# Thirteen u tiles instead of nine ahead of the gate matmuls, and a third, moved buffer for spilled activations

## The chip, the core and the metric

The kernel is one program on one core of a Trainium2 chip. Its engines run side by side and each works through its own instructions in order: TensorE (PE; its weight loads are PEld), VectorE (DVE), ScalarE (ACT), GpSimd (POOL) and SyncE (SP, which issues most DMAs). Engines wait for each other and for DMAs by semaphores. A DMA issued by ScalarE or GpSimd stands in that engine's order too. The metric is the device time of one execution in microseconds; shown are a median over runs and one execution with a profile.

## The reference

Two layers over 512 tokens of width 1024: a recurrent block, then attention, each followed by an expert layer ("PEER"). The expert layer picks 16 of 128 x 128 single-neuron experts per head and token and sums them:

```python
def peer(h, w_q, sub_keys, u_tab, v_tab):
    q = (h @ w_q).reshape(B, S, PEER_HEADS, 2, PEER_HALF)
    s = jnp.einsum('bshpd,hpnd->bshpn', q, sub_keys).astype(jnp.float32)
    v1, i1 = lax.top_k(s[..., 0, :], PEER_TOPK)
    v2, i2 = lax.top_k(s[..., 1, :], PEER_TOPK)
    cand = (v1[..., :, None] + v2[..., None, :]).reshape(B, S, PEER_HEADS, PEER_TOPK * PEER_TOPK)
    cv, ci = lax.top_k(cand, PEER_TOPK)
    ...
    idx = e1 * N_KEYS + e2
    g = jax.nn.softmax(cv, axis=-1).astype(h.dtype)
    def experts(args):
        hc, ic, gc = args
        act = jax.nn.gelu(jnp.einsum('bcd,bchkd->bchk', hc, u_tab[ic]), approximate=False)
        return jnp.einsum('bchk,bchkd->bcd', gc * act, v_tab[ic])
```

There are 8 heads, 128 keys, 16384 experts per layer, and everything is float32.

## The kernel before, in words

The expert layer treats the 512 tokens in two ways. For the last block of 128 tokens it gathers the chosen rows of the tables u and v, one choice per step: an indirect DMA on GpSimd's queue (L1113) fills a buffer `grow` (four of them), VectorE takes the dot product with the token (L1117) or adds the weighted row (L1120, L1122). There are 256 such steps per layer, `total`; `done` counts those emitted. For the other three blocks (384 tokens) it computes all 16384 experts densely and multiplies them with a matrix of gate weights that is zero where an expert was not chosen.

A u tile is 128 experts: its weights are loaded by SP into `raw` (four buffers), ScalarE rounds them to `whi` and VectorE takes the rest `wlo` (three buffers each, shared with `vh` and `vl` of the second half), TensorE makes 8 x 3 matmuls of 384 columns into one of two PSUM banks named `u` (L187 to L189), and ScalarE applies the gelu into SBUF. Of the 128 tiles the first 8 go into the space of x, tiles 8 to 16 and those from 93 on stay in SBUF, and tiles 17 to 92 (`SPILL` = 76) are spilled: the gelu writes a small tile `gsp` (L895), and ScalarE issues a DMA of it to scratch memory `gscr` (L896), from which SP fetches it in the second half (L1035).

An expert layer runs in these stages.

- Queries, scores and top-k, four groups; after each group some u tiles (`UPQ`), 23 in all. The last block's indices are decoded first, so that the gathers can begin.
- `UDEC` u tiles, with `FIRST` gather steps spread among them, while VectorE decodes the three dense blocks. When block 0 is decoded, three transposes into `et` (L808) bring its indices and weights into the gate layout.
- 24 gate groups of 16 tokens. VectorE builds one-hot tiles `oo` and weighted ones `pr` (L835, L837, two buffers each), TensorE multiplies them into PSUM `wps` (L843), ScalarE evicts four banks into `stg` (L846) and issues the DMA to `wscr` (L848). The u tiles up to number 88 and the gather steps up to `EARLY` are spread over the groups, as is the decoding of blocks 1 and 2.
- `UEND` = 5 more u tiles.
- The second half: for each of the 128 tiles t, `weigh` multiplies the activation with its gate weights and splits it (`ah`, `al`), `v_load` loads and splits v (`vh`, `vl`), and TensorE adds 18 matmuls into the six banks `acc` (L187 to L189 again). Gate weights come from `wscr` as `wt`, for eight tiles at a time, two buffers (L993); tiles 0 and 1 use a small tile `wfirst` (L989). The u tiles from 93 on and the remaining gather steps run among the tiles; all gather steps are spread by weights from `done` to `total`.

The order on each engine is made by a scheduler, from the order of the source, priorities and its own timeline of the instructions. Tiles live in pools that lie on a stack: `gath` (gpool), `cg`, and above them `dec` (dpool), with the pool of the current stage on top. `dec.close()` frees dpool after the first half, and the pool `vp` of the second half (`wt`, `ah`, `al`) is laid over the freed space; a tile there waits until what lay in its place has been read. gpool stays to the end of the layer.

Of the kernel before, what the change touches and what calls it, by code (L numbers as in the profile page):

```python
# [9 lines left out]
F32 = mybir.dt.float32  # L10
# [11 lines left out]
P = 128  # L22
# [17 lines left out]
ND = 3 * P  # L40
# [2 lines left out]
SPILL = 76  # L43
LEAD = KC + RING - 3 + SPILL
UPQ = (5, 6, 6, 6)
UDEC = 9
UEND = 5
FIRST = 12
EARLY = 100
HT = 8  # L50
RAWS = 4
GROWS = 4
# [29 lines left out]
class Trunk:  # L82
# [768 lines left out]
    def peer(self, l):  # L851
        nc, io, tc = self.nc, self.io, self.tc
        nd = NB - 1
        with ExitStack() as st:
# [28 lines left out]
            def u_part(after=None):  # L883
                t = state["u"]
                state["u"] = t + 1
                out = self.bank("u", True)
                hi, lo = self.wtile(io["uT"][l][t], KC, eng=nc.vector)
                with tc.issue_after(after) if after is not None else ExitStack():
                    for k, (bh, bl) in enumerate(h):
                        self.mm3(out[:, :ND], (hi[:, k, :], lo[:, k, :]), (bh[:, :ND], bl[:, :ND]), k == 0, k == KC - 1)  # L890
                if t < KC:
                    gact[t] = self.x[:, t, :ND]
                elif LEAD - SPILL <= t < LEAD:
                    g = gpool.tile([P, ND], F32, name="gsp", bufs=2)
                    nc.scalar.activation(g, out[:, :ND], AF.Gelu)  # L895
                    nc.scalar.dma_start(self.gscr[l, t - (LEAD - SPILL)], g)  # L896
                    return
                else:
                    gact[t] = acts.tile([P, ND], F32, name="gact")
                nc.scalar.activation(gact[t], out[:, :ND], AF.Gelu)  # L900

            gpool = st.enter_context(tc.tile_pool(name=f"gath{l}", bufs=1))
# [7 lines left out]
            dpool = dec.enter_context(tc.tile_pool(name=f"dec{l}", bufs=1))  # L910

            def decodes(bs):
                for b in bs:
                    res = []
                    for _ in self.decode(dpool, cvs[b], cis[b], iu[b], res):
                        yield
                    if b == nd:
                        gsel.append(self.gather_index(gpool, l, *res))
                    else:
                        prep[b] = self.gate_prep(pool, *res)  # L920

            with tc.tile_pool(name=f"pq{l}", bufs=1) as pool:
                for grp in range(4):
# [29 lines left out]
                    for _ in range(UPQ[grp]):  # L953
                        u_part()
            with tc.tile_pool(name=f"gate{l}", bufs=1) as pool:
                nsg = P // TG
                steps = decodes(range(nd))
                for i in range(UDEC):
                    u_part()
                    while done < FIRST * (i + 1) // UDEC:  # L960
                        next(gsteps)
                        done += 1
                while 0 not in prep:
                    next(steps)
                n0, nt = state["u"], nd * nsg
                ds = 0
                wlast = [None, None]
                for i in range(nt):
                    while state["u"] < n0 + (LEAD - UEND - n0) * (i + 1) // nt:
                        u_part(after=wlast[-2])  # L970
                    wlast.append(self.gate_group(pool, l, i // nsg, i % nsg, *prep[i // nsg]))
                    while ds < 7 * (i + 1) // nsg:
                        next(steps, None)
                        ds += 1
                    while done < min(EARLY, FIRST + (EARLY - FIRST) * (i + 1) // (nt - 2)):
                        next(gsteps)
                        done += 1
                while state["u"] < LEAD:
                    u_part(after=wlast[-1])
# [248 lines left out]
```

## Time and profile before

| | |
|---|---|
| median of three runs | 3194.11 us (3189.2 to 3195.05) |
| the profiled execution | 3191.91 us, its span 3190.1 us |
| mean granted TensorE clock | 0.973 |
| TensorE, VectorE, ScalarE, GpSimd busy | 3003.0, 2582.8, 1379.5, 859.8 us |
| DMA | 821.13 MB, 257 GB/s over the span |

Layer 0's expert layer lies from about 213 us to 1531 us of the span, layer 1's from about 1857 us to 3167 us. A busy share is an average over stages with different limits, so the stages are read apart. In a row on waits, what stands before the arrow waited, and what stands behind it ended the wait; in a timeline row, the bracket at the end holds the idle time before an instruction and what ended it.

### The profile page before, as it was taken

How to read it: one execution, taken by the hardware profiler on the slowest of the kernel's cores; microseconds unless marked ns; L12 is line 12 of the kernel's file. 1: busy time of each engine (PE TensorE's matmuls, PEld its weight loads, DVE VectorE, ACT ScalarE, POOL GpSimd, SP SyncE). 2: the span in 40 equal slices, each digit the busy share in tenths (PEclk: the TensorE clock that was granted, in tenths of full speed). 3: DMA queues.
4: the chain of work that ended last, by engine and by line, in shares of the span. 5: the costliest groups of instructions: out<-in, count | busy, mean ns of one | idle time of the engine just before them, and what ended most of it. 6: DMA issues, size and time to landing. Idle time of an engine off the chain costs nothing.

```text
span 3190.1 us, 43195 instructions
## 1 busy us (share of the span) xinstructions
PE 3003.0 (94%) x15334; PEld 2633.5 (83%) x15334; DVE 2582.8 (81%) x4927; ACT 1379.5 (43%) x1960; POOL 859.8 (27%) x653
## 2 busy tenths in 40 slices
PE   6999987999999999999889889969998999999997
PEld 5659987998877889998667679969998788889996
DVE  8859999987788877878578878998986677778776
ACT  5533244655333333333566542445554333333333
POOL 0000014433122114443356500034333111124440
PEclk9999998999999999999999999989999999999999
DMA  7444578998999999998113244479998999999994
GB/s 287 148 161 139 176 240 296 343 321 301 316 333 359 350 337 317 329 334 284 52 50 112 67 156 130 150 263 329 335 314 297 308 319 301 313 310 333 319 324 142
DMA packets 345110, 821.13 MB, mean 257 GB/s; under 512 B 33600, under 2 KB 179136, under 8 KB 338496
## 3 DMA queue, kind: packets, MB, share of 16 engines
q1 hardware_dynamic: 239632, 460.91, 43.7%
q0 software_dynamic: 73728, 268.47, 24.2%
q10 hardware_dynamic: 31536, 89.00, 7.4%
q8 instruction: 121, 1.98, 0.2%
q14 instruction: 93, 0.76, 0.1%
HBM read 730.98 MB, written 87.29 MB: 257 GB/s over the span
## 4 chain that ended last, share of the span: by engine, by line
PE 77%; DVE 11%; DMA 4%; ACT 4%; issue 3%; POOL 1%; ACTq 0%; SPq 0%; DVEq 0%; POOLq 0%
PE acc L187 10%; PE acc L188 10%; PE acc L189 10%; PE u L187 10%; PE u L188 9%; PE u L189 9%; PE wps L843 5%; PE pq L187 2%; PE pq L189 2%; PE pq L188 2%; DVE wlo L163 1%; PE wo L207 1%; DMA grow<-in_u_dram,idx 1%; ACT stg L846 1%; DVE ada_junk L151 1%
## 5 line engine op out<-in xcount | busy, mean ns | idle before, releaser
L1113 POOL DMA_INDIRECT grow<-in_u_dram,idx x256 | 340.6, 1330 | 1416.8 <-DVE oh L791 704.1
L187 PE MATMUL u<-hh,wlo 128*128 128x384 f32 x2048 | 696.4, 340 | 21.7 <-ACT gsp L895 21.7
L189 PE MATMUL u<-hh,whi 128*128 128x384 f32 x2048 | 692.3, 338 | 0.0
L188 PE MATMUL u<-hl,whi 128*128 128x384 f32 x2048 | 691.5, 338 | 0.0
L188 PE MATMUL acc<-vl,ah 128*128 128x512 f32 x1536 | 601.0, 391 | 0.4 <-DVE vl L163 0.4
L189 PE MATMUL acc<-vh,ah 128*128 128x512 f32 x1536 | 600.6, 391 | 0.0
L187 PE MATMUL acc<-vh,al 128*128 128x512 f32 x1536 | 563.5, 392 | 12.4 <-ACT vh L162 7.5
L1113 POOL DMA_INDIRECT grow<-in_v_dram,idx x256 | 350.9, 1371 | 680.0 <-DVE gacc L1122 467.9
L163 DVE TENSOR_TENSOR vl<-vraw,vh 128x1024 fp32r<-128x1024 f32 x256 | 313.5, 1225 | 194.3 <-ACT vh L162 189.0
L163 DVE TENSOR_TENSOR wlo<-raw,whi 128x1024 fp32r<-128x1024 f32 x307 | 376.8, 1227 | 112.7 <-ACT whi L162 105.8
L162 ACT ACTIVATE whi<-raw 128x1024 fp32r<-128x1024 f32 (+2 forms) x364 | 350.1, 963 | 220.3 <-PE u L189 128.8
L187 PEld LDWEIGHTS u<-hh,wlo 128*128 128x128 f32 x2048 | 389.5, 190 | 29.9 <-ACT gsp L895 27.0
L188 PEld LDWEIGHTS u<-hl,whi 128*128 128x128 f32 x2048 | 389.1, 190 | 2.9
L189 PEld LDWEIGHTS u<-hh,whi 128*128 128x128 f32 x2048 | 388.6, 190 | 0.0
L187 PEld LDWEIGHTS acc<-vh,al 128*128 128x128 f32 x1536 | 289.9, 189 | 73.2 <-ACT vh L162 8.9
L189 PEld LDWEIGHTS acc<-vh,ah 128*128 128x128 f32 x1536 | 289.5, 189 | 60.6
L188 PEld LDWEIGHTS acc<-vl,ah 128*128 128x128 f32 x1536 | 289.5, 188 | 59.8 <-DVE vl L163 0.8
L162 ACT ACTIVATE ah<-gact 128x384 fp32r<-128x384 f32 x240 | 125.8, 524 | 483.8 <-PE acc L189 308.6
L1117 DVE CUSTOM_DVE_ANT_0 grow<-grow,hn 128x1024 f32<-128x1024 f32 x256 | 308.8, 1220 | 31.1 <-DMA grow<-in_u_dram,idx 31.0
L1122 DVE SCALAR_TENSOR_TENSOR gacc<-grow,gdot,gacc 128x1024 f32<-128x1024 f32 x254 | 325.2, 1280 | 1.6 <-DMA grow<-in_v_dram,idx 0.6
L162 ACT ACTIVATE vh<-vraw 128x1024 fp32r<-128x1024 f32 x256 | 268.9, 1050 | 117.6 <-issue 45.3
L846 ACT ACTIVATE stg<-wps 128x512 f32<-128x512 f32 x192 | 190.9, 1094 | 70.8 <-PE wps L843 66.8
(337 smaller groups left out, 4232.1 us busy)
## 6 DMA issues: line engine op xcount, KB each, us to landing
raw<-in_uT_dram SPq DMA_DIRECT2D x256, 512.0 KB
vraw<-in_v_dram SPq DMA_DIRECT2D x256, 512.0 KB
ada_raw<-in_adaw_dram SPq DMA_DIRECT2D x112, 512.0 KB
wscr<-stg ACTq DMA_DIRECT2D x48, 1024.0 KB
wt<-wscr SPq DMA_DIRECT2D x32, 1536.0 KB
gscr<-gsp ACTq DMA_DIRECT2D x152, 192.0 KB
gact<-gscr SPq DMA_DIRECT2D x152, 192.0 KB
raw<-in_w_pq_dram SPq DMA_DIRECT2D x32, 512.0 KB
```

Source lines behind the costliest of these rows:

```text
L151: nc.vector.tensor_tensor_reduce(junk, raw, self.csil, op0=OP.mult, op1=OP.add, scale=1.0, scalar=b, accum_out=col)
L162: nc.scalar.activation(hi, src, AF.Copy)
L163: return (eng or nc.vector).tensor_tensor(lo, src, hi.bitcast(F32), op=OP.subtract)
L187: nc.tensor.matmul(out, al, bh, start=first, stop=False)
L188: nc.tensor.matmul(out, ah, bl, start=False, stop=False)
L189: return nc.tensor.matmul(out, ah, bh, start=False, stop=last)
L207: self.nc.tensor.matmul(outs[m], ws[k][:, m, :], acts[k], start=k == 0, stop=k == KC - 1)
L843: last = nc.tensor.matmul(wps[:, t * P:t * P + P], oo[:, n4 + a, :, t], pr[:, q * n4 + a, :, t], start=q == 0, stop=q == 1)
L846: nc.scalar.activation(stg[:, :, c:c + 4].rearrange("p e t -> p t e"), wps.rearrange("p (t e) -> p t e", t=4), AF.Copy, scale=1.0 / GSCALE)
L1113: nc.gpsimd.indirect_dma_start(out=row, out_offset=None, in_=tabs[s], in_offset=bass.IndirectOffsetOnAxis(ap=idx[:, k:k + 1], axis=0))
L1117: nc.vector.tensor_tensor_reduce(row, row, hn, op0=OP.mult, op1=OP.add, scale=1.0, scalar=0.0, accum_out=col)
L1122: nc.vector.scalar_tensor_tensor(acc, row, col, acc, op0=OP.mult, op1=OP.add)
```

## The change

Nine u tiles between the scores and the gate matmuls become thirteen (`UDEC`), and the u tiles that remain for the gate groups are four fewer. Of the gather steps, 4 and not 12 are asked for in that place (`FIRST`), and 94 and not 100 up to the end of the gate groups (`EARLY`), so six more per layer fall into the second half. The tile `gsp` has three buffers and not two, and they are taken from dpool and not from gpool.

```diff
-UDEC = 9
+UDEC = 13
 UEND = 5
-FIRST = 12
-EARLY = 100
+FIRST = 4
+EARLY = 94
...
                 elif LEAD - SPILL <= t < LEAD:
-                    g = gpool.tile([P, ND], F32, name="gsp", bufs=2)
+                    g = dpool.tile([P, ND], F32, name="gsp", bufs=3)
                     nc.scalar.activation(g, out[:, :ND], AF.Gelu)
                     nc.scalar.dma_start(self.gscr[l, t - (LEAD - SPILL)], g)
                     return
```

How this moves instructions shows at three places. The first lies between the scores and the gate groups of layer 0. On ScalarE (`et` and `gt` are the transposed indices and weights of block 0, the first thing that the gates need):

```order
+L794 ACTIVATE ib<-i4f 128x1024
+L895 ACTIVATE gsp<-u 128x384
+L162 ACTIVATE whi<-raw 128x1024
+L896 DMA gscr<-gsp 128x384
 L811 ACTIVATE et<-et 128x2x16x8
 L814 ACTIVATE gt<-et 128x128
```

Four such triples of gelu, rounding and scratch write now stand ahead of `et`; on TensorE the u tiles between the last score and the first gate matmul go from 19 to 23 in either layer, and some three of them stand between the transposes of `et`. On VectorE, at the same place (`e` is the decoded index for which these transposes wait, L1117 a gather step):

```order
 L773 SCALAR_TENSOR_TENSOR off<-row,off 128x128
-L800 TENSOR_TENSOR e_4019<-oh 128x64
-L1117 ISA grow,gdot<-grow,hn 128x1024
-L1117 ISA gdot 128x1
+L163 TENSOR_TENSOR wlo<-raw,whi 128x1024
+L1117 ISA grow,gdot<-grow,hn 128x1024
+L1117 ISA gdot 128x1
+L800 TENSOR_TENSOR e_4131<-oh 128x64
 L791 TENSOR_TENSOR oh<-iota_m,rc 128x1024
```

The split of a new u tile and a gather step stand ahead of `e` now. Up to the first gate product, VectorE has four splits more; the gather steps ahead of it are 15 where they were 16 in layer 0, and 15 as before in layer 1.

The second place is ScalarE in the last third of layer 0's gate groups. Before:

```order
L162 ACTIVATE whi<-raw 128x1024 x2
L846 ACTIVATE stg<-wps 128x4x128 x2
L895 ACTIVATE gsp<-u 128x384
L846 ACTIVATE stg<-wps 128x4x128 x2
L896 DMA gscr<-gsp 128x384
L895 ACTIVATE gsp<-u 128x384
L848 DMA wscr<-stg 128x2048
L896 DMA gscr<-gsp 128x384
```

and with the change:

```order
L895 ACTIVATE gsp<-u 128x384
L162 ACTIVATE whi<-raw 128x1024
L846 ACTIVATE stg<-wps 128x4x128
L896 DMA gscr<-gsp 128x384
L846 ACTIVATE stg<-wps 128x4x128 x3
L848 DMA wscr<-stg 128x2048
L895 ACTIVATE gsp<-u 128x384
```

Before, two roundings stand together ahead of the evictions and the gelus behind them; now gelu and rounding alternate up to the end of the gate groups, as they did before in the first two thirds.

The third place is the passage to the second half of layer 0, on ScalarE, with what each row waits for in brackets (DMAHW0 to DMAHW7 count landed DMAs, the others an engine's instructions). Before:

```order
L895 ACTIVATE gsp<-u 128x384 [waits DMAHW5_49]
L896 DMA gscr<-gsp 128x384 [waits Activation_49]
L162 ACTIVATE ah<-x 128x384 [waits DVE_49]
L162 ACTIVATE vh<-vraw 128x1024 [waits DMAHW4_49,PE_49]
```

and with the change:

```order
L162 ACTIVATE vh<-vraw 128x1024 [waits DMAHW1_49,DVE_49,PE_49]
L895 ACTIVATE gsp<-u 128x384 [waits DMAHW2_49]
L896 DMA gscr<-gsp 128x384 [waits Activation_49]
L162 ACTIVATE ah<-x 128x384 [waits DMAHW4_49,DMAHW1_49,DMAHW7_49,DMAHW0_49,DVE_49]
L162 ACTIVATE ah<-x 128x384 [waits DVE_49]
```

Before, the first `ah` stood ahead of the last two `gsp` and waited for VectorE alone. Now it stands behind the last one, and three of the DMAs it waits for are scratch writes of `gsp`, the last tile's among them. On SP, the first load of `wt` waited for the last gate matmul, and now for the last `gsp` and its scratch write as well, before:

```order
L993 DMA wt<-wscr 128x24x128 [waits DMAHW0_49,PE_49]
L993 DMA wt<-wscr 128x24x128 [waits DMAHW1_49]
```

and with the change:

```order
L993 DMA wt<-wscr 128x24x128 [waits DMAHW1_49,DMAHW0_49,DMAHW5_49,PE_49,Activation_49]
L993 DMA wt<-wscr 128x24x128 [waits DMAHW6_49]
```

The second `wt` load of each pair follows the first in either program.

## The prediction, on record before the changed kernel was timed

> **What bounds the kernel now.** I read the page first, then the busy times by stage, then the waits, then the two places where a wait stands on TensorE.
>
> ```profile
> span 3190.1 us, 43195 instructions
> PE 3003.0 (94%) x15334; PEld 2633.5 (83%) x15334; DVE 2582.8 (81%) x4927; ACT 1379.5 (43%) x1960; POOL 859.8 (27%) x653
> PE 77%; DVE 11%; DMA 4%; ACT 4%; issue 3%; POOL 1%; ACTq 0%; SPq 0%; DVEq 0%; POOLq 0%
> ```
>
> TensorE is busy for 94% of the span and is 77% of the chain that ended last, so the time is its work plus its holes. Next, the first half of each expert layer by stages: from the last score to the first gate matmul (388.4 to 499.7 in layer 0, 2033 to 2137.4 in layer 1), the gate matmuls, and the u tiles after the last of them up to the first output matmul; columns are length, then busy time of each engine, granted clock, DMA share, GB/s.
>
> ```profile
> core 0: us, PE busy (x) PEld busy (x) DVE busy (x) ACT busy (x) POOL busy (x), PEclk, DMA share, GB/s
> 388.40:499.70 111.30, 79.88 (x458) 78.98 (x458) 104.93 (x359) 47.02 (x60) 25.49 (x20) 0.86 0.71 232
> 499.70:813.00 313.30, 306.87 (x1975) 299.63 (x1975) 270.87 (x311) 171.63 (x209) 122.50 (x75) 0.97 0.91 319
> 813.00:838.60 25.60, 21.44 (x121) 20.48 (x119) 14.30 (x15) 8.89 (x12) 7.55 (x6) 1.00 1.03 338
> 2033.00:2137.40 104.40, 80.02 (x458) 78.90 (x457) 100.03 (x351) 45.28 (x58) 22.43 (x19) 0.91 0.68 225
> 2137.40:2450.00 312.60, 306.66 (x1974) 298.27 (x1973) 267.29 (x307) 174.19 (x210) 117.46 (x74) 0.98 0.90 317
> 2450.00:2490.00 40.00, 28.77 (x145) 27.81 (x144) 19.19 (x19) 10.11 (x14) 12.12 (x10) 0.91 1.00 336
> ```
>
> Before the first gate matmul VectorE is the bound (104.9 of 111.3 us, 100.0 of 104.4) and TensorE stands still for 31.4 and 24.4 us. In the gate stage it is the other way round, TensorE 306.9 of 313.3 us. The waits name the holes; columns are total, times, longest.
>
> ```profile
> PE et L808 <- DVE e L800: 33.1, 4, 13.3
> PE wps L843 <- DVE pr L837: 22.5, 2, 12.4
> PE u L187 <- ACT gsp L895: 21.7, 17, 2.6
> ```
>
> The first two rows, 55.6 us, are the holes before the gates: the transposes wait for the decoded indices, the first gate matmul for its one-hot product. The third is spread over the last third of the gates and the u tiles behind them: a u tile waits until the gelu of an earlier one has emptied its PSUM bank.
>
> **Term A, the hole before the gates.** What one u tile and one gather cost:
>
> ```profile
> 412.00:462.00 50.00, 50.00 (x290) 50.00 (x289) 5.91 (x12) 1.00 0.69 216
> L163 DVE TENSOR_TENSOR wlo<-raw,whi 128x1024 fp32r<-128x1024 f32 x19 | 23.5, 1235 | 0.0
> L1117 DVE CUSTOM_DVE_ANT_0 grow<-grow,hn 128x1024 f32<-128x1024 f32 x16 | 19.4, 1215 | 5.2 <-DMA grow<-in_u_dram,idx 5.2
> L1122 DVE SCALAR_TENSOR_TENSOR gacc<-grow,gdot,gacc 128x1024 f32<-128x1024 f32 x254 | 325.2, 1280 | 1.6 <-DMA grow<-in_v_dram,idx 0.6
> ```
>
> The first row counts u matmuls alone: 290 in 50 us, 0.172 us each, 24 to a tile, so 4.14 us; four more tiles put 16.6 us of work into each hole. They also put four splits of 1.24 us, 4.9 us, on VectorE ahead of the first gate product. The table asks for eight fewer gathers there, but the order takes one out in layer 0 (16 to 15) and none in layer 1 (15 to 15): the gathers fill places that the scheduler has free anyway. So the first gate matmul comes 4.9 - 1.2 = 3.7 us later in layer 0 and 4.9 us later in layer 1, and the gate stage has 16.6 us less to do: a gain of 12.9 + 11.7 = 24.6 us. Bounds: 33.2 us if VectorE takes the splits in its own idle 6.4 and 4.4 us; 14 us if each new split costs twice its time because its load comes late (the gather row shows 5.2 us of such waits). I take the middle, since VectorE is 94 to 96% busy there, and its idle is in waits for the first gathers.
>
> **Term B, the late gates.** The gate stage after the change holds 290 us of TensorE work and, with 75 gather steps down to 70 (74 to 71) and a split less, 263 us of VectorE work: 91%, where it was 86%. An early stretch of it, then the late ones:
>
> ```profile
> 520.00:680.00 160.00, 160.00 (x1047) 157.12 (x1046) 145.09 (x174) 94.38 (x115) 69.44 (x39) 1.00 0.94 336
> 720.00:813.00 93.00, 86.57 (x541) 83.05 (x540) 72.93 (x74) 47.43 (x58) 27.61 (x21) 0.93 0.87 299
> 2360.00:2450.00 90.00, 84.09 (x523) 80.48 (x521) 68.94 (x72) 44.91 (x55) 29.16 (x20) 0.94 0.85 297
> 794.51 2.80 ACT L846 ACTIVATE stg<-wps 128x512 f32<-128x512 f32 x3
> 797.72 0.49 ACT L895 ACTIVATE gsp<-u 128x384 f32<-128x384 f32 x1 [0.40 <-ACT stg L846]
> 798.26 0.69 PE L187 MATMUL u<-hh,wlo 128*128 128x384 f32 x1 [2.50 <-ACT gsp L895]
> ```
>
> With VectorE at 91% from 520 to 680, TensorE had no hole, and DMA went at 336 GB/s; so the denser gates can hold. The late ones have holes although VectorE has slack: the gelu at 797.72 stands behind three evictions of gate banks on ScalarE, and TensorE waits 2.50 us for it. In the new order each gelu stands directly behind its tile to the end of the stage, as it stood in the stretch without holes. Of the 21.7 us of these waits nearly all lie here. The clock adds to it: 0.93 over 93 us, 0.94 over 90 and 0.91 over 40 us make 2 x (0.07 x 93 + 0.06 x 90 + 0.09 x 40) = 31 us at half rate; with some 12 of them idle, 19 us of work at half rate lose 9. Together 30 us; against it I put 5 us of new holes per layer for the fuller VectorE. B is a gain of 20 us, bounds 30 and 0 (as many new holes as old ones).
>
> **Term C, the passage to the second half.** Here the moved buffer costs. The second half's pool lies where the decode pool was. In the new program the first load of gate weights (wt) and the first split of an activation (ah) wait for the scratch write of the last spilled tile; before, they stood ahead of it. The last gelu itself stands behind the third vh, which waits for the last u matmul. Rows that carry it:
>
> ```profile
> 838.63 1.66 PE L187 MATMUL acc<-vh,al 128*128 128x512 f32 x6 [1.15 <-ACT vh L162]
> 844.21 0.97 PE L187 MATMUL acc<-vh,al 128*128 128x512 f32 x3 [1.20 <-ACT vh L162]
> 2490.02 1.22 PE L187 MATMUL acc<-vh,al 128*128 128x512 f32 x2 [5.16 <-ACT vh L162]
> L162 ACT ACTIVATE vh<-vraw 128x1024 fp32r<-128x1024 f32 x256 | 268.9, 1050 | 117.6 <-issue 45.3 <-DMA vraw<-in_v_dram 24.5 <-PE acc L189 23.0
> 2477.73 0.33 ACTq L896 DMA_DIRECT2D gscr<-gsp  x1
> 2045.72 2.21 DMA gscr<-gsp
> SPq L1035 <- DMA gscr<-gsp: 24.6, 6, 7.0
> L163 DVE TENSOR_TENSOR al<-gact,ah 128x384 fp32r<-128x384 f32 x240 | 135.1, 563 | 71.4 <-ACT ah L162 71.0 <-issue 0.2
> L998 DVE TENSOR_TENSOR gact<-gact,wt 128x384 f32<-128x384 f32 x240 | 132.6, 552 | 0.0
> 2462.62 25.79 DMA wt<-wscr
> 2600.00:2700.00 100.00, 100.00 (x443) 82.81 (x442) 0.00 (x0) 0.00 (x0) 1.00 0.93 309
> ```
>
> Now 1.15 + 1.20 and 5.16 us are lost. After, counted from the end of the last u tile: vh 1.05, gelu 0.49, issue 0.33, the write between 2.2 us (the chain) and 7.0 us (the longest wait of SP for one), where I take 4.5, then ah and al, 0.5 to 0.6 each: the first output matmul at about 8 us. Tiles 0 and 1 need no wt and last 2 x 18 matmuls of 0.226 us (443 in 100 us), 8.1 us, to 16 us. The wt load starts at 6.4 us. Its price lies between 4.7 us (1536 KB at the 336 GB/s above) and 25.8 us (the chain's piece, two loads and gathers together); I take 11, near half of that piece. Behind it come the product 0.55, ah and al, a split and a gather that stand between on VectorE: tile 2 at about 21 us, a second hole of 4 to 5 us. With 2 us at half rate that is 14 us per layer, 28 in all, against 7.5 us and some 1.5 us of slow clock now: a loss of 19 us. Bounds: 5.2 us per layer and no second hole, a loss of 2; or 10 + 20 + 4 us per layer, a loss of 59. The near end is likelier than the far one, which counts two loads for one.
>
> [...]
>
> **Term D, the second half.** Six gather steps per layer move there, 1.22 to 1.28 us each on VectorE and 512 KB of DMA.
>
> ```profile
> 838.60:1530.80 692.20, 685.72 (x3202) 591.18 (x3203) 556.98 (x756) 255.64 (x345) 201.02 (x156) 0.99 0.94 326
> 2490.00:3167.10 677.10, 677.08 (x3178) 585.22 (x3179) 514.43 (x662) 246.74 (x337) 182.99 (x154) 1.00 0.89 302
> ```
>
> VectorE has 135 and 163 us idle here and TensorE none, so 7.5 us per layer hide under TensorE; without that cover they would cost 15. Layer 0 is denser (326 GB/s, 6.5 us of holes already): I put 1 us, bounds 0 and 5. The rest of the program differs by a few exchanged neighbours; I price it at nothing.
>
> **Sum.** -24.6 - 20 + 19 + 1 = -24.6 us, from the profiled execution's 3191.9 us to 3167.3, so 3167. The median shown is 2.2 us above that execution, the three runs reach from 3189.2 to 3195.05.
>
> **The rivals.** First, the passage eats the gain and more. It is one mechanism: wt cannot start before the last scratch write, lands late among gathers and v loads, and all output matmuls from tile 2 stand behind it. At the far bound: 3191.9 - 24.6 - 20 + 59 + 1 = 3207. It turns the result slower once the holes exceed 26 us per layer. For it: the 25.8 us piece. Against: that piece held two loads of wt, three of v and gathers. Second, the gates keep their pace: if VectorE in order sets it, the 16.6 us taken out of TensorE there become holes. Then A is a loss of 8.6 (the later first gate) and B a gain of 10 (the tail's waits): 3192 + 8.6 - 10 + 19 + 1 = 3210. For it: VectorE at 91%. Against: at 91% it held TensorE full from 520 to 680, and its own waits there are for TensorE. Third, the passage is cheap and the late gates close fully: 3191.9 - 24.6 - 30 + 2 + 1 = 3140. For it: the 2.21 us write.
>
> **How the numbers follow.** The forecast (3153 to 3187) has 0.65, the cheap passage (below 3153) 0.17, the dear passage 0.11, the gates that keep their pace 0.07. The bounds of A and C reach over 3143 to 3190, which leaves out the far ends of three rivals, about 2 in 10. A measurement of this kernel tells no less than 0.2%, 6.4 us, from no change. Faster by more: forecast, cheap passage and a fifth of the dear one's cases, 0.84; the rest of that one and the slow gates are split into 0.07 within and 0.09 slower.
>
> **What would show it.** A: the first gate matmul 3 to 5 us later after the last score, 23 u tiles before it and not 19, TensorE's hole there 18 and 13 us. B: the wait of u for gsp below 5 us in all, the clock near 1.00 up to the last gate. C: the first output matmul waits about 8 us behind the last u tile and a second hole stands before the third v tile, with ah or wt behind the scratch write as releaser. D: no new hole after that. A hole before a gate product in the middle of the stage would prove B wrong, a passage under 5 us or over 25 us C.

## The result, and the profile after

The changed kernel takes 3175.0 us (median of 5 runs, 3172.0 to 3175.4); the kernel before took 3194.1 us beside it (5 runs, 3189.0 to 3202.0). The ratio is 0.9931, 95% interval 0.9917 to 0.9945: faster by 0.7%, and 8 us slower than the 3167 forecast, inside its range of 3153 to 3187. The page of the changed kernel, span and busy times:

```profile
span 3171.8 us, 43218 instructions
PE 2997.4 (95%) x15334; PEld 2626.9 (83%) x15334; DVE 2585.5 (82%) x4927; ACT 1377.0 (43%) x1960; POOL 860.7 (27%) x653
```

The same work, 18.3 us less span than before. Busy times by stage, with the columns as in the prediction: the stage before the gates, the gates, the u tiles up to the first output matmul, for layer 0 and layer 1; then the second halves, and last the attention part between the layers:

```profile
386.90:502.10 115.20, 96.71 (x554) 95.50 (x553) 108.20 (x362) 50.87 (x66) 26.51 (x19) 0.94 0.72 248
502.10:799.70 297.60, 293.06 (x1928) 287.20 (x1928) 260.27 (x302) 170.55 (x208) 113.09 (x69) 0.99 0.92 319
799.70:832.90 33.20, 20.81 (x120) 20.50 (x119) 20.20 (x21) 9.28 (x14) 11.05 (x7) 0.85 0.93 314
2028.10:2136.60 108.50, 96.22 (x554) 95.39 (x554) 104.21 (x354) 50.93 (x66) 24.14 (x19) 0.96 0.72 249
2136.60:2437.70 301.10, 292.63 (x1928) 286.86 (x1928) 261.93 (x304) 170.12 (x208) 109.47 (x69) 0.98 0.90 318
2437.70:2468.70 31.00, 20.80 (x121) 20.51 (x120) 18.80 (x19) 9.47 (x14) 12.81 (x10) 0.88 0.92 304
832.90:1517.00 684.10, 676.31 (x3154) 580.43 (x3155) 557.51 (x757) 252.75 (x338) 207.90 (x162) 1.00 0.94 331
2468.70:3148.70 680.00, 675.77 (x3154) 582.94 (x3155) 514.42 (x664) 242.29 (x331) 188.69 (x159) 0.99 0.89 306
1517.00:1851.50 334.50, 287.66 (x1337) 217.89 (x1335) 258.97 (x473) 193.50 (x405) 165.01 (x134) 0.92 0.23 76
```

and the attention part of the kernel before:

```profile
1530.80:1856.80 326.00, 279.32 (x1337) 213.50 (x1335) 253.66 (x473) 192.87 (x405) 166.26 (x134) 0.94 0.25 78
```

From the last score to the last output matmul, layer 0 took 1142.4 us and takes 1130.1 (386.9 to 1517.0); layer 1 took 1134.1 and takes 1120.6. That is -25.7 us in the layers the change touches, where the forecast had -24.6. The attention part, which it doesn't touch, took 326.0 us and takes 334.5: +8.5 us, and with 1 us less elsewhere the span's 18.3.

TensorE's waits, as totals, times and longest in us:

```profile
PE wps L843 <- DVE pr L837: 31.8, 8, 9.9
PE acc L187 <- DVE al L163: 30.6, 8, 12.4
```

No wait of u for gsp is left (21.7 us before). The waits of et and of the first product fell with the two holes before the gates, from 31.4 and 24.4 us to 18.5 (115.2 less 96.7) and 12.3 (108.5 less 96.2). Eight waits of acc for al, 30.6 us, stand where two of 4.9 us stood, 28.2 us of them in four holes at the two passages. New are waits for pr in the middle of the gates, the largest of them here with VectorE's rows just before it:

```profile
2246.63 3.60 PE L843 MATMUL wps<-pr,oo 128*128 128x128 f16 x29 [8.23 <-DVE pr L837]
...
2241.46 0.28 DVE L818 TENSOR_TENSOR gp<-gt,gp 128x128 f16<-128x128 f32 x1
...
2242.80 1.22 DVE L1117 CUSTOM_DVE_ANT_0 grow<-grow,hn 128x1024 f32<-128x1024 f32 x1
...
2244.14 1.22 DVE L1117 CUSTOM_DVE_ANT_0 grow<-grow,hn 128x1024 f32<-128x1024 f32 x1
...
2245.40 2.33 DVE L837 TENSOR_TENSOR pr<-oo,gp 128x2048 f16<-128x2048 f16 x2
```

This is the switch from block 0 to block 1: the first product of block 1 needs its weights `gp`, which are decoded, transposed and ready at 2241.7. VectorE has no idle time of over half a microsecond in the ten before the product, and a split and two gather steps stand between `gp` and it. In all kernels of this document the holes of over 1.3 us before gate products, after the first product, stand at such a switch, 101 to 112 us or 206 to 225 us after the first gate matmul; the one exception is 2.4 us long, in the change with two buffers. In the kernel before, the four switches take 8.9 to 12.3 us from the last product of one block to the first of the next, and u matmuls fill them; in the changed kernel they take 11.2 to 16.8 us, and the u matmuls leave holes of 2.8, 1.1, 8.2 and 0.2 us in them. Late in the gates, where the waits for gsp had been, TensorE is now full at full clock:

```profile
720.00:799.70 79.70, 79.15 (x527) 77.22 (x527) 65.84 (x71) 44.34 (x54) 24.68 (x17) 1.00 0.92 318
2360.00:2437.70 77.70, 77.70 (x520) 75.81 (x519) 64.67 (x69) 43.98 (x54) 23.07 (x17) 1.00 0.92 327
```

The passage of layer 1, in order of time by engine (TensorE, ScalarE, VectorE, SP); a bracket is the idle time before and what ended it:

```profile
2468.68 0.76 PE L187 MATMUL acc<-vh,al 128*128 128x512 f32 x1 [10.20 <-DVE al L163]
2482.70 0.80 PE L187 MATMUL acc<-vh,al 128*128 128x512 f32 x1 [4.22 <-DVE al L163]
...
2459.99 0.33 ACTq L896 DMA_DIRECT2D gscr<-gsp  x1
2464.27 0.94 ACT L162 ACTIVATE ah<-x 128x384 fp32r<-128x384 f32 x2 [4.31 <-DMA gscr<-gsp]
...
2460.75 2.60 DVE L1122 SCALAR_TENSOR_TENSOR gacc<-grow,gdot,gacc 128x1024 f32<-128x1024 f32 x2
2463.27 1.02 DVE L998 TENSOR_TENSOR x<-x,wfirst 128x384 f32<-128x384 f32 x2
2464.20 1.28 DVE L1122 SCALAR_TENSOR_TENSOR gacc<-grow,gdot,gacc 128x1024 f32<-128x1024 f32 x1
2466.82 1.29 DVE L1122 SCALAR_TENSOR_TENSOR gacc<-grow,gdot,gacc 128x1024 f32<-128x1024 f32 x1 [1.34 <-DMA grow<-in_v_dram,idx]
2468.03 1.02 DVE L163 TENSOR_TENSOR al<-x,ah 128x384 fp32r<-128x384 f32 x2
2478.35 1.03 DVE L998 TENSOR_TENSOR x<-x,wt 128x384 f32<-128x384 f32 x2 [9.30 <-DMA wt<-wscr]
...
2464.22 8.25 SPq L993 DMA_DIRECT2D wt<-wscr  x2
```

The last u matmul ends at 2458.5. The scratch write of the last spilled tile is issued at 2460.0 and frees ah 4.3 us later. But two gather steps on VectorE keep the weighting of tile 0, which ah needs too, until 2463.8, so without the write ah could have come less than half a microsecond sooner. Then al does not follow: two more gather steps stand ahead of it on VectorE, the second waiting 1.34 us for its row. The wt load is issued at 2464.2, and its product starts at 2478.35, 14.1 us later, so the third tile finds a second hole. Layer 0 has holes of 12.41 and 1.41 us, and there ah waits for VectorE alone (ScalarE's row, then VectorE's):

```profile
827.08 0.99 ACT L162 ACTIVATE ah<-x 128x384 fp32r<-128x384 f32 x2 [5.10 <-DVE x L998]
...
823.98 2.60 DVE L1122 SCALAR_TENSOR_TENSOR gacc<-grow,gdot,gacc 128x1024 f32<-128x1024 f32 x2
826.50 1.02 DVE L998 TENSOR_TENSOR x<-x,wfirst 128x384 f32<-128x384 f32 x2
...
831.06 1.28 DVE L1122 SCALAR_TENSOR_TENSOR gacc<-grow,gdot,gacc 128x1024 f32<-128x1024 f32 x1 [2.35 <-DMA grow<-in_v_dram,idx]
832.26 1.02 DVE L163 TENSOR_TENSOR al<-x,ah 128x384 fp32r<-128x384 f32 x2
```

As in layer 1, two gather steps stand ahead of the weighting of tiles 0 and 1, and two more between it and al, here with a wait of 2.35 us for a row.

### The profile page after: what moved, and what is told of

It reads as the page before. It is cut to its first block, busy times and chain, and to the rows that moved or that the text cites. A ratio compares the mean times of both kernels' runs of the same rounds, so it can differ in the third digit from the quotient of the medians.

```text
span 3171.8 us, 43218 instructions
## 1 busy us (share of the span) xinstructions
PE 2997.4 (95%) x15334; PEld 2626.9 (83%) x15334; DVE 2585.5 (82%) x4927; ACT 1377.0 (43%) x1960; POOL 860.7 (27%) x653
## 4 chain that ended last, share of the span: by engine, by line
PE 74%; DVE 11%; issue 6%; DMA 5%; ACT 2%; POOL 2%; DVEq 0%; SPq 0%; POOLq 0%; ACTq 0%
PE acc L187 10%; PE acc L188 10%; PE acc L189 10%; PE u L187 9%; PE u L188 9%; PE u L189 9%; PE wps L843 5%; PE pq L187 2%; PE pq L188 2%; PE pq L189 2%; DVE wlo L163 1%; PE wo L207 1%; DMA ada_raw<-in_adaw_dram 1%; DMA grow<-in_u_dram,idx 1%; DVE grow L1117 1%
## 5 line engine op out<-in xcount | busy, mean ns | idle before, releaser
L187 PE MATMUL acc<-vh,al 128*128 128x512 f32 x1536 | 573.7, 392 | 33.4 <-DVE al L163 30.6
L187 PEld LDWEIGHTS acc<-vh,al 128*128 128x128 f32 x1536 | 289.5, 189 | 96.7 <-issue 23.8
L1122 DVE SCALAR_TENSOR_TENSOR gacc<-grow,gdot,gacc 128x1024 f32<-128x1024 f32 x254 | 324.8, 1279 | 9.8 <-DMA grow<-in_v_dram,idx 8.5
L1117 DVE CUSTOM_DVE_ANT_0 grow<-grow,hn 128x1024 f32<-128x1024 f32 x256 | 309.1, 1219 | 25.8 <-DMA grow<-in_u_dram,idx 25.6
L843 PE MATMUL wps<-pr,oo 128*128 128x128 f16 x1536 | 190.5, 297 | 31.8 <-DVE pr L837 31.8
```

The costliest lines, as they stand in the source:

```text
L187: nc.tensor.matmul(out, al, bh, start=first, stop=False)
L843: last = nc.tensor.matmul(wps[:, t * P:t * P + P], oo[:, n4 + a, :, t], pr[:, q * n4 + a, :, t], start=q == 0, stop=q == 1)
L1117: nc.vector.tensor_tensor_reduce(row, row, hn, op0=OP.mult, op1=OP.add, scale=1.0, scalar=0.0, accum_out=col)
L1122: nc.vector.scalar_tensor_tensor(acc, row, col, acc, op0=OP.mult, op1=OP.add)
```

## Experiments

The table puts the runs together. Lost time is the time in which TensorE does nothing plus half of its busy time in windows of half clock, both layers added, worked out from the instructions and the granted clock of each trace. The first column reaches from the last score to the first gate matmul, the gates from there to the end of the last u tile of the first half, the passage from there to 25 us after the first output matmul. The attention part is its whole length. Two rows are second executions of a program with no edit: what the columns differ by there is scatter, some 1 us before and in the gates, up to 3 at the passage and 3 to 5 in the second half.

| kernel | median us | ratio to before (95%) | lost: before gates | gates | passage | second half | attention part |
|---|---|---|---|---|---|---|---|
| before | 3194.1 | | 56.7 | 38.8 | 9.0 | 10.0 | 326.0 |
| before, second execution | 3192.9 (one run) | | 56.1 | 39.9 | 9.6 | 6.8 | 327.9 |
| the change | 3175.0 | 0.9931 (0.9917-0.9945) | 31.1 | 20.0 | 34.6 | 6.4 | 334.5 |
| the change, second execution | 3170.5 (two runs) | 0.9917 (0.9898-0.9937) | 29.8 | 20.2 | 31.7 | 10.9 | 330.2 |
| tiles alone | 3167.9 | 0.9909 (0.9893-0.9926) | 31.7 | 39.3 | 5.6 | 12.5 | 331.8 |
| buffer alone | 3190.1 | 0.9984 (0.9975-0.9994) | 56.6 | 8.8 | 35.4 | 6.5 | 330.4 |
| gathers alone | 3191.4 | 0.9986 (0.9976-0.9997) | 57.7 | 34.8 | 6.7 | 8.9 | 337.1 |
| tiles and gathers | 3163.7 | 0.9898 (0.9880-0.9915) | 32.2 | 36.0 | 7.5 | 9.5 | 331.6 |
| the change, two buffers | 3175.6 | 0.9934 (0.9913-0.9954) | 31.0 | 40.7 | 20.7 | 8.2 | 334.4 |
| ring | 3157.2 | 0.9876 (0.9860-0.9893) | 30.7 | 20.6 | 20.4 | 8.9 | 331.5 |
| ring, UEND 7 | 3173.2 | 0.9918 (0.9899-0.9937) | 30.4 | 43.2 | 16.7 | 11.4 | 332.8 |
| ring, EARLY 84 | 3149.3 | 0.9850 (0.9832-0.9868) | 30.6 | 22.4 | 14.8 | 4.5 | 330.1 |
| ring, EARLY 74 | 3148.3 | 0.9853 (0.9832-0.9875) | 31.2 | 20.7 | 2.1 | 13.7 | 334.3 |
| ring, EARLY 74, UDEC 16 | 3145.5 | 0.9834 (0.9815-0.9853) | 16.3 | 34.5 | 7.6 | 9.3 | 334.1 |

The ratios are what to compare: the median of the kernel before was 3194.1 to 3198.5 us beside them.

### One part of the change at a time

The tiles:

```diff
-UDEC = 9
+UDEC = 13
```

> The kernel before with UDEC 13 alone (four more u tiles before the first gate matmul; the table of gathers and the buffers of the spilled activations stay). My theory (terms A and B): the hole before the gates shrinks to 18 and 13 us with 23 u tiles before the first gate product, which comes 4 to 5 us later, gain 24.6 us; the waits of u for gsp in the late gates stay near 20 us, since there are still two buffers in the first pool; the passage to the second half stays at 2 and 5 us. Time before less 25, 3169, and less than the whole change's 3175 by what the passage costs there, if the buffer pays for itself no more than that. Rival: the tiles pay only with the third buffer, because u tiles in the holes write spilled activations faster than two buffers empty; then new waits of u for gsp stand in the holes, these stay at 31 and 24 us, and the time stays above 3185.

3167.9 us, as expected, and no slower than the whole change: 0.2% below it, with intervals that overlap. The hole before the gates fell by the same 25 us as in the whole change, 56.7 to 31.7. The late gates were a surprise: the waits for gsp fell to half without the buffer,

```profile
PE u L187 <- ACT gsp L895: 10.1, 6, 2.0
```

but the lost time of the gates stayed at 39 us, because holes of 3.9, 6.4 and 1.7 us before the first gate products of blocks 1 and 2 came in their place.

The buffer:

```diff
-                    g = gpool.tile([P, ND], F32, name="gsp", bufs=2)
+                    g = dpool.tile([P, ND], F32, name="gsp", bufs=3)
```

> The kernel before with the spilled activations in three buffers of the decode pool alone (19 u tiles before the first gate product, the table of gathers as it was). My theory (terms B and C): waits of u for gsp fall from 21.7 us to below 5, the clock of the late gates rises, gain 20 to 25 us; the passage to the second half then costs 12 to 14 us per layer of holes, 16 to 20 us lost over both; together 3194 less 5, 3185 to 3192. Rival: the third buffer is what makes the change faster; 3175 to 3180. Second rival: the passage alone decides; 3205 or more.

3190.1 us, within the first theory's range. The gates gain 30.0 us of lost time and the passage costs 26.4, nearly the whole of it. So the buffer by itself is worth 5 us (0.16%, interval 0.06 to 0.25%).

The table of gathers:

```diff
-FIRST = 12
-EARLY = 100
+FIRST = 4
+EARLY = 94
```

> The kernel before with FIRST 4 and EARLY 94 alone (the table asks for eight fewer gathers between the scores and the gate matmuls). My theory: the order leaves 16 and 15 gathers before the first gate product as it was, so nothing moves there and the time is 3194 within 6 us. Rival: eight gathers of 1.22 us leave VectorE there, the first gate matmul comes 10 us earlier in each layer; 3175.

3191.4 us, nothing moved before the gates (57.7 us lost, 56.7 before), and the rival's 10 us per layer are not there. The gain of 0.14% is at the edge of what its interval tells from none; in the lost time it comes out of the gates and the passage, 4 and 2 us, the second within the scatter.

### The pairs

The change with the old buffers, that is the tiles and the gathers without the third part (edit against the changed kernel):

```diff
-                    g = dpool.tile([P, ND], F32, name="gsp", bufs=3)
+                    g = gpool.tile([P, ND], F32, name="gsp", bufs=2)
```

> The changed kernel with the spilled activations back in two buffers of the first pool: four more u tiles and eight fewer gathers, no third buffer. The tiles alone gave 3168 where the whole change gives 3175. My theory: the buffer's move costs the difference, since its passage (13.8 and 14.4 us of holes) costs more than its late gates bring once the tiles have taken most of those waits away (10.1 us of u for gsp left with the tiles alone). Then 3163 to 3170 here, holes of 2 to 5 us per layer at the passage and some 10 us of waits of u for gsp. Rival: the eight gathers that are shifted to the second half cost it, where the waits of acc for vl and al stand; then 3173 to 3178 here.

3163.7 us: the buffer's move costs the changed kernel some 10 us (0.9931 less 0.9898; 7 by the two runs of the changed kernel timed beside it, 3169.2 and 3171.8 against 3160.1 to 3166.8), and the rival falls. TensorE's wait of u for gsp in this kernel:

```profile
PE u L187 <- ACT gsp L895: 6.6, 4, 2.0
```

With 19 u tiles before the gates the buffer gained 30.0 us of lost time in the gates; with 23 it gains 16.0 (36.0 to 20.0), since the holes before the products at the block switches stay. The passage costs 26.4 and 27.1 (24 by the second execution of the changed kernel).

The change with two buffers in the new place:

```diff
-                    g = dpool.tile([P, ND], F32, name="gsp", bufs=3)
+                    g = dpool.tile([P, ND], F32, name="gsp", bufs=2)
```

> The changed kernel with two buffers for the spilled activations in the decode pool, not three. It has the changed kernel's passage (theory: 12 to 14 us of holes per layer, from the place alone) and the late gates of two buffers (waits of u for gsp some 10 us, with their slow clock another 5 to 10): 3180 to 3190. Rival: the third buffer does nothing, only the place counts, since the later order of the gelus comes from the place: 3175 within 4, with waits of u for gsp below 3 us.

```profile
PE acc L187 <- DVE al L163: 16.9, 3, 8.2
PE u L187 <- ACT gsp L895: 9.6, 6, 2.0
```

The time, 3175.6, is the rival's, but not for its reason: the waits for gsp are there as the theory had them, 9.6 us, and the gates lose 40.7 us where three buffers lose 20.0. The passage is cheaper instead, 20.7 and not 34.6 us. So the place alone costs 13 us at the passage (7.5 to 20.7); the third buffer brings 20.7 us in the gates and, by the order that the scheduler then makes, costs 14 more at the passage (11 by the second execution).

### The passage

The last three spilled tiles of each layer are written into the ring of kept activations and spilled from there, so that the last write no longer holds the second half's pool:

```diff
-                    g = dpool.tile([P, ND], F32, name="gsp", bufs=3)
+                    if t >= LEAD - 3:
+                        g = acts.tile([P, ND], F32, name="gact")
+                    else:
+                        g = dpool.tile([P, ND], F32, name="gsp", bufs=3)
```

> The changed kernel, but the last three spilled tiles of each layer are put into the ring of kept activations (tile gact) and not into the decode pool, from where they are written out as before. Then the first wt load and the first ah of the second half wait for the scratch write of the fourth-last spilled tile and not of the last. My theory (term C): the two holes at the passage, 12.4 and 1.4 us in layer 0, 10.2 and 4.2 us in layer 1, with the half-rate windows behind them, fall to 3 to 6 us per layer, and the time to some 3155 (3150 to 3160). Rival: the holes are the wt load and the gathers that it lands among, whatever it waited for; or the tiles in the ring delay the first kept activations instead; 3172 to 3176.

3157.2 us, as expected and 0.55% below the change (0.4% by its second timing). The lost time of the passage fell from 34.6 to 20.4 us, less than expected: the second holes, where wt had waited for the write, are gone (5.6 us), but first holes of 8.68 and 7.47 us are left of 12.41 and 10.20. The lines of the program from the edit on are three higher here, L1001 for L998 and L1125 for L1122. TensorE's wait ("issue" means that the profile shows nothing that it waited for), VectorE's rows in layer 1 before it, where the last u matmul ends at 2452.5, and ScalarE's first ah in layer 0:

```profile
PE acc L187 <- issue: 16.2, 2, 8.7
```

```profile
2455.67 2.60 DVE L1125 SCALAR_TENSOR_TENSOR gacc<-grow,gdot,gacc 128x1024 f32<-128x1024 f32 x2
2458.18 1.02 DVE L1001 TENSOR_TENSOR x<-x,wfirst 128x384 f32<-128x384 f32 x2
2459.32 1.03 DVE L163 TENSOR_TENSOR al<-x,ah 128x384 fp32r<-128x384 f32 x2
...
827.02 0.99 ACT L162 ACTIVATE ah<-x 128x384 fp32r<-128x384 f32 x2 [5.48 <-DVE x L1001]
```

The first ah waits for VectorE and not for a scratch write. What is left is the order on VectorE: two gather steps ahead of the first tiles' weighting, 2.6 us, and then that weighting, ah and al one after the other. The gather steps that stood between ah and al in the changed kernel are gone. So the loss in the changed kernel was two things, the write, which held back wt, and the order that the scheduler makes around it, which set most of the first hole.

To get the first weighting done under u matmuls, two more u tiles were put behind the last gate (edit against the ring kernel):

```diff
-UEND = 5
+UEND = 7
```

> The kernel with the last three spilled tiles in the ring of kept activations, and UEND 7 instead of 5: two more u tiles behind the last gate matmul. There the third part of the first weights (wfirst) and the products of tiles 0 and 1 stand ahead of the gathers on VectorE, so the holes that are left at the passage (8.7 and 7.5 us, with 10 and 7 us of half clock) close to 1 to 3 us each: theory, a gain of 12 to 18 us, 3140 to 3146. Rival: the gate stage loses 8.3 us of u matmuls per layer and VectorE, at 259 of 297 us, sets its pace: the holes before its products grow by as much, and the time stays at 3154 to 3160.

3173.2 us: the rival, and beyond it.

```profile
PE wps L843 <- DVE pr L837: 48.1, 8, 9.6
```

The passage's holes before the first output matmul closed to 3.6 and 3.3 us, but the waits for pr rose from 31.1 to 48.1 us and the gates' lost time from 20.6 to 43.2. The gate stage is as long as in the ring kernel (300.6 and 300.0 us against 297.6 and 302.0) with 8.3 us less TensorE work in it: the four block switches have holes of 5.6 to 8.0 us now, so they and not TensorE's work set its length.

Then fewer gather steps in the gates (edit against the ring kernel):

```diff
-EARLY = 94
+EARLY = 84
```

> The kernel with the last three spilled tiles in the ring of kept activations, and EARLY 84 instead of 94: ten more gather steps of each layer go from the gates to the second half. Theory: in the gate stage VectorE sets the pace (259 of 297 us, holes before its products of 4 and 8 us, and gathers stand ahead of the first output tile's products at the passage); 12.5 us less of it there closes half of these holes or more, and the second half, with 125 and 157 us idle on VectorE, takes them: 3145 to 3153. Rival: the second half of layer 0 already loses 9 us in holes before output matmuls, and grows by as much as the gates gain: 3155 to 3162.

and twice as many, `EARLY = 74`:

> The same with EARLY 74: twenty steps per layer moved. If VectorE in the gates is the cause of the holes that are left there, they are gone with this at the latest (below 3 us in all), and the time is 3140 to 3150; under the rival (the second half pays) it is 3160 or more and above the one with 84.

3149.3 and 3148.3 us, 0.26 and 0.23% below the ring kernel (the intervals of the ratios overlap, the runs, 3145.7 to 3154.8 against 3155.7 to 3158.6, do not), but the theory's reason falls. The gates lose 22.4 and 20.7 us, as with 94, and the holes before products in layer 0 are the same: 2.83 and 1.12, then 2.81 and 1.11. The gate stages of the EARLY 74 kernel, and of the ring kernel in layer 1:

```profile
502.00:798.00 296.00, 292.08 (x1925) 286.68 (x1923) 258.78 (x309) 169.97 (x207) 94.58 (x56) 0.99 0.86 301
2130.10:2431.20 301.10, 294.48 (x1927) 288.95 (x1927) 249.46 (x286) 169.83 (x207) 97.52 (x59) 0.97 0.86 300
```

```profile
2129.70:2431.70 302.00, 293.78 (x1927) 287.41 (x1927) 261.95 (x304) 169.71 (x208) 114.91 (x69) 0.98 0.90 317
```

In layer 0 VectorE is nearly as busy as it was (258.8 us, 260.3 in the ring kernel): the scheduler filled the freed places with other work that was due later, such as the position tables. In layer 1, where there are none, it has 12.5 us less, and the lost time is still 13 us in both. So 12.5 us less load on VectorE does not remove these holes. Each stands at a block switch and ends with a product on VectorE; what makes the switch longer than the u matmuls there stays open. The gain that is clear of the scatter is at the passage, 20.4 to 14.8 and 2.1 us. With 74, al of tile 0 lies before the end of the last u tile, and the first output matmul starts without a wait:

```profile
815.25 0.61 DVE L163 TENSOR_TENSOR al<-x,ah 128x384 fp32r<-128x384 f32 x1 [0.25 <-ACT ah L162]
...
818.66 0.39 PE L187 MATMUL acc<-vh,al 128*128 128x512 f32 x1
```

Layer 0's second half loses 13.7 us with 74 and 4.5 with 84, where it lost 8.9 in the ring kernel; two executions of the changed kernel differ as much (6.4 and 10.9), so whether it pays, as the rival had it, is not shown.

Three more u tiles on that, `UDEC = 16`:

> The kernel with the ring and EARLY 74, and UDEC 16 instead of 13: three more u tiles before the first gate matmul. The holes there are still 18.5 and 12.4 us. By the working that held for the first four tiles, three more put 12.4 us of TensorE work into each hole and 3.7 us of splits on VectorE ahead of the first gate product: holes of 9 to 10 and 3 to 4 us, a gain of 8.7 us per layer, 17 in all: 3131 to 3139. Rival: the gate stage, then with 282 us of TensorE work beside 248 to 258 us of VectorE, turns to VectorE's pace and gives it back in holes before its products: 3145 or more.

3145.5 us, the lowest of all, though its interval doesn't tell it from the one with 13. The holes before the gates fell to 11.9 and 4.4 us, and the gates lost 14 us more, most of it in one hole in layer 1 and one of 6.89 us in layer 0:

```profile
2246.62 1.59 PE L843 MATMUL wps<-pr,oo 128*128 128x128 f16 x12 [11.70 <-DVE pr L837]
```

Both stand at block switches. This is the rival's time: the term that had held for four tiles stops where the gates hand the gain back.

### The attention part

Two programs were profiled a second time with no edit, for the part that the change does not touch:

> The changed kernel itself, a second profiled execution, for the part between the two expert layers (from the last output matmul of layer 0 to the first pq matmul of layer 1). It took 326.0 us before and 334.5 us after with the same matmuls and the same holes, but 27 and 44 us of windows at half clock. [...] Rival: the changed order of instructions costs it: 334 to 335 again. [...]

> The kernel before itself, a second profiled execution, for the part between the two expert layers. It took 326.0 us with 27 us at half clock; nine profiles of seven other orders (the changed kernel twice: 334.5 and 330.2) lie at 330.2 to 337.1. [...] Rival: the order of instructions before makes it short, and it is 326 within 1 us again.

The second execution of the changed kernel, then the second of the kernel before, then the kernel with the gathers alone:

```profile
1520.40:1850.70 330.30, 283.79 (x1338) 215.54 (x1335) 256.03 (x473) 193.02 (x405) 166.26 (x134) 0.93 0.24 77
```

```profile
1526.50:1854.40 327.90, 280.07 (x1336) 213.52 (x1334) 253.90 (x472) 192.95 (x405) 165.54 (x134) 0.95 0.24 77
```

```profile
1525.00:1862.10 337.10, 288.39 (x1337) 219.66 (x1335) 259.44 (x473) 193.30 (x405) 165.23 (x134) 0.92 0.23 76
```

The changed kernel came out at 330.2 us here (3170.5 in time), 4.3 below its first profiled execution; the kernel before at 327.9, 1.9 above. In TensorE's and VectorE's rows of this part the kernels with the gathers alone and the changed one have one order, and with 337.1, 334.5 and 330.2 they span 7 us. The idle time is 46 to 49 us in the three rows. What differs is busy time with the same matmuls (283.8 us in the second execution of the changed kernel, 287.7 in its first, 288.4 with the gathers alone), at a mean clock of 0.93 in the first of these and 0.92 in the others. So most of the 8.5 us was scatter, and the rivals' figures, 334 to 335 for the changed kernel and 326 within 1 us for the kernel before, did not come again. Whether the new order adds something stays open: the two executions of the old order, 326.0 and 327.9, are the shortest of all, but four kernels that are one row apart from it on TensorE have 331.6 to 334.4 (the tiles and gathers, the change with two buffers, UEND 7, EARLY 74), and two with the changed kernel's order there 330.4 and 330.1 (the buffer alone, EARLY 84).

## Why the prediction was right, and where it was not

Stage by stage the four terms come to -24.6 as forecast and -25.7 as measured in the layers. The second executions of both kernels give -25.6. The single terms, as lost time from the table, add up to -22.4; the other 3 us are less busy time of TensorE at full clock, which no run explains:

**A, -24.6 forecast, -25.6 measured.** The first gate matmul comes 3.9 and 4.1 us later after the last score (forecast 3.7 and 4.9), with 23 u tiles before it, and the holes are 18.5 and 12.3 us (18 and 13). The tiles alone show the same 25 us, and the gathers alone leave the place as it was, which was the reading of the order. With three more tiles the same step holds for most of the holes, and the gates take it back.

**B, -20 forecast, -18.8 measured.** The step is right in sum by luck, since two errors cancel. The old waits and their slow clock were 38.8 us, not 30: half clock cost 17 us and not 9. The new holes were put at 5 us per layer and are 4.5 and 8.5 us idle with 7 us of slow clock, 20 in all. That "a hole before a gate product in the middle of the stage would prove B wrong" was too sharp: the holes of 2.83, 1.11 and 8.23 us are there, and the sum stands. They stand at the block switches, which the working did not look at. The rival of the gates that keep their pace was near: in the kernel with UEND 7, two u tiles further, the gates keep their length. But 12.5 us less of VectorE's work (layer 1 with EARLY 74) did not shorten them. The rival put this down to VectorE's pace over the whole stage; the runs show it at the switches.

**C, +19 forecast, +25.6 measured (+22 by the second executions).** The mis-sized term. Before it was 9.0 us, as forecast; after, 34.6 (31.7) and not 28. The wait for the scratch write is there in layer 1, 4.3 us where 4.5 were taken, and the ring kernel, which takes it away, wins 14 us of lost time. But the chain of the first hole was only in part the one named: the working let ah wait for the write and al follow at 0.5 to 0.6 us each, and counted VectorE's order for tile 2 alone. In either layer two gather steps stand ahead of the weighting that ah waits for and two more between ah and al, so the first hole is 12.4 and 10.2 us and not 8, and in the ring kernel, without the write, it still is 8.7 and 7.5. That 8 was near is luck. The second hole, 1.4 and 4.2 us, is the forecast 4 to 5 in layer 1 alone; its chain, wt behind the write, is right, since it goes with the write. In layer 1 the wt load took 14.1 us from issue to product where 11 were put, and the dear passage's 25.8 us is not seen.

Half clock after these holes costs 1.9 us in layer 0 and 4.5 in layer 1; the 2 us per layer of the working were the author's estimate. The profile of the changed kernel has a median of 4.9 us from issue to landing for all 152 scratch writes of gsp, and the chain's 2.21 us, on which the cheap passage rested, is less than half of that.

**D, +1 forecast, -3.6 measured, and +4.1 by the second executions.** The moved gathers cost nothing that stands out of this scatter.

**What was priced at nothing** is the attention part, and there the time was missed: it came out 8.5 us longer in the first profiled execution, 3173.6 us, which is more than its whole distance from 3167. In the second executions it is 2.3 us longer, and the changed kernel takes 3169.2 us there. So most of the miss in the time is scatter. That the layers came within 1 us of the forecast is in part luck too: what C missed, 6.6 us, is met by D's scatter and the 3 us of busy time.

**Bounds.** The 3143 and 3190 that the prediction gives as the reach of A and C do not follow from its terms: their near ends together make 3142, their far ends 3218.

**What the prediction did not ask** is whether the change should be taken as a whole. B and C were computed as two terms, but both belong to one edit, the buffer, and their sum was -1. The runs show the rest: B's gain is 30.0 us with 19 tiles and 16.0 with 23, and the passage costs 24 to 27 in both, so the same edit is worth -5 us alone and +7 to +10 in the whole. Tiles and gathers without it would have given 3164.

## What to carry to other kernels

Add up a change by its edits and not only by its stages: an edit whose gain and loss lie in different stages can turn sign with the edits beside it, here when the tiles opened holes at the block switches that the buffer does not close. When a buffer is moved into a pool that a later pool overlays, look for its last writer, count what the scheduler puts behind it on every engine between its release and the next stage's first instruction, and give the last few tiles another place if one is free. Items taken off an in-order engine by a scheduler's table can be replaced by other work, so see where the waiting instruction stands after it, and not how busy the engine is.

## Of the hardware, not expected

In the attention part a hole of one and a half microseconds was followed by half clock in one execution and not in another. Here is the same instruction after the same hole, with the hole just before it, in the two executions of the changed kernel, the first and then the second:

```profile
1550.59 0.73 PE L187 MATMUL lat<-hmh,wlo 128*128 128x512 f32 x2 [0.45 <-ACT hmh L162]
...
1553.34 0.72 PE L188 MATMUL lat<-hml,whi 128*128 128x512 f32 x1 [1.54 <-DVE hml L163]
```

```profile
1554.03 0.74 PE L187 MATMUL lat<-hmh,wlo 128*128 128x512 f32 x2 [0.46 <-ACT hmh L162]
...
1556.77 0.50 PE L188 MATMUL lat<-hml,whi 128*128 128x512 f32 x1 [1.53 <-DVE hml L163]
```

In the first the granted clock is 0.51 from 1553.40 to 1556.81, after 1.00 in the 16.8 us before, and the 128x512 matmuls behind the instruction start 0.43 us apart there and 0.23 us apart from 1557.1 on. In the second the instruction takes 0.50 us where it took 0.72. The holes are as long in either, 0.45 and 1.54 us in the first, 0.46 and 1.53 in the second, so their length does not tell the two executions apart; what does was not shown.

The attention part held 27 us of half clock in the first execution of the kernel before and 44 in that of the changed one (the last window, which both have, left out), at mean clocks of 0.94 and 0.92; in the second executions the mean clock was 0.95 and 0.93, and the idle time is 46 to 48 us in all four. This is a floor on what one profile of this program can show: the changed kernel took 334.5 and 330.2 us there.
